# A hybrid RWKV-7 layer on one core: gathered blocks in two buffers, their scaling on VectorE, and seven products that nothing reads in the recurrence's merge

## The chip, the cores and the metric

The kernel runs on one core of a Trainium2 chip. The metric is the device time of one execution in microseconds (us), as the median of three runs. A profiled execution gives the trace from which the rows below come.

## What is computed

One decoder layer for 4096 tokens of 1024 channels in float32. The reference, cut to its steps:

```python
proj = x @ w_in
pool_out = multiscale_pool(proj[..., :256], pool_w, pool_scale)
rwkv_out = rwkv7_mix(proj[..., 256:], ...)        # 12 heads of 64
mixed = concat([pool_out, rwkv_out]) @ w_out
h = layer_norm(alpha * x + mixed)
y = layer_norm(alpha * h + hierarchical_moe(h))   # top group of 4, two of its 8 experts

# inside rwkv7_mix, per head and token; state is 64 x 64
sa = einsum('bhij,bhj->bhi', state, -kk)
state = state * decay + sa * (kk * a) + v * k
out = einsum('bhij,bhj->bhi', state, r)
# afterwards: a norm over each head, + sum(r * k * r_k) * v (the bonus), * a gate
```

## The kernel before, in words

The program has four phases, and the trace shows them one after the other: `phase_project` (to about 1060 us; x @ w_in, each float32 operand split in a high and a low part), `phase_rwkv` (1060 to 2432 us; the recurrence), `phase_out` (w_out, the first layer norm, the router), `phase_moe` (the experts and the last norm).

The recurrence is computed in chunks of 64 tokens. A **unit** is 256 tokens (4 chunks) of one of two groups of 6 heads (3 pairs), so there are 16 x 2 = 32 units. Inside a chunk the tokens depend on one another through a triangular 64x64 matrix for each head, which has to be inverted. Each unit goes through these pieces:

- `load` reads r, k, v and the decays; `gate` computes the low-rank products; `prep` builds the scaled operands AR and KB (VectorE lines 383 to 434), multiplies them on TensorE (L443) and masks the products into G (L445, VectorE). G is written to DRAM (L450, SyncE's queue).
- At the end of `prep` stands `invert`. Four DMAs gather the 32x32 diagonal blocks of G from DRAM, 24 partitions each, into a tile `gi` of 96 partitions (L481), which has one buffer. GpSimd (POOL) scales a unit matrix and the blocks by the norms rn (L483 writes `db`, 96x512; L484 scales `gi`, 96x1024) and then inverts the blocks by elimination: 31 steps, each one multiplication (L489) and one addition (L491).
- `merge` puts the inverses together: `db` goes to DRAM (L500) and back as `ut` (L506), VectorE transposes a part (L509 writes `w`), 24 tiny products (L521), ACT copies the result into W (L529), 24 more (L524), VectorE copies into Uf (L531). With that the 64x64 inverses stand in `ut`.
- `values`, `tail` and `chunk` run the recurrence, chunk by chunk. A `chunk` has three pieces: products of the state with AR (L592, L597), the products with the inverse (L601, with L575 of the next chunk between them), the update of the state (L608 on TensorE, L610 and L611 on VectorE) and the output (L613).
- `bonus` computes the sum of r, k and r_k times v (L462, L469, L470); `post` the norm over a head, the gate and the write of the result.

The engines' order is written out by hand. Every piece is a generator that stops at places (`yield`); tables of ticks (`LOAD`, `GATE`, `PREP`, `BONUS`, `MERGE`, `POST`, `TAIL`, `VALUES`, `CHUNK`) give each stop a tick, with 96 ticks to a unit and 24 to a chunk. All pieces are sorted by tick and recorded one after the other, and each engine works through its own instructions in this order; DMAs stand in the queue of the engine that issues them, most of them SyncE's (SP). An instruction that waits holds up all that stands behind it on its engine.

At the start of `phase_out` the tables that the router and the experts fill later get their first content: 128 rows of zeros for `d_h` and `d_acc` (0.5 MB each), 1 MB of `d_tab`, and `d_gtab`. The weights w_out come in pieces of 512 KB through a pool of two buffers (`o_ws`), issued by ACT, between whose loads ACT also issues the norm's and router's parameters.

Of the kernel before, what the change touches and what calls it, by code (L numbers as in the profile page):

```python
# [27 lines left out]

def phase_project(tc, A, rkv, lora, mixT, xsp):


    nc = tc.nc
# [5 lines left out]
    with ExitStack() as ctx:  # L38
# [38 lines left out]
        def cols(g):  # L77
# [4 lines left out]
            return c  # L82

        wpool = ctx.enter_context(tc.tile_pool(name="pj_wr", bufs=1))
        for g in range(2):
# [110 lines left out]

LOAD = [-5, 92]
GATE = [-63]
PREP = [-76, -70, -67, -67, -62, -62, -55, -55, -48, -36, -31, -31, -30, -23, -17, -15, -15, -15, -13, -7, 3, 4, 7, 7, 7, 7, 8, 28, 30, 30]
BONUS = [7, 13, 19]  # L200
MERGE = [50, 82, 94, 94, 101, 101]
POST = [-2, -2, 11, 11, 20, 23, 35, 37, 49, 50, 57, 60, 62]
TAIL = [-1]
VALUES = [-43]
CHUNK = [0, 6, 12]

def phase_rwkv(tc, A, rkv, lora, mixT, gsc, dsc, rsc):
# [8 lines left out]
    with ExitStack() as ctx:  # L216
# [136 lines left out]
        def prep(n):  # L353
# [493 lines left out]
def bcast_row(ap, n):  # L847

    return bass.AP(tensor=ap.tensor, offset=ap.offset, ap=[[0, 128], [1, n]])


def phase_out(tc, A, mixT, hrow, acc, tab, gtab, plan):
# [3 lines left out]
    with ExitStack() as ctx:  # L856

        wop = ctx.enter_context(tc.tile_pool(name="o_wo", bufs=1))
        cst = ctx.enter_context(tc.tile_pool(name="o_c", bufs=1))
        wst = ctx.enter_context(tc.tile_pool(name="o_w", bufs=2))  # L860
        mp = ctx.enter_context(tc.tile_pool(name="o_m", bufs=3))
# [63 lines left out]
        nc.gpsimd.iota(token, pattern=[[128, NQ]], base=0, channel_multiplier=1)  # L925

        z = cst.tile([128, D], F32, name="zrow")
        nc.gpsimd.memset(z, 0.0)
        nc.sync.dma_start(hrow[S:], z)
        nc.sync.dma_start(acc[S:], z)  # L930
        ft = cst.tile([128, 128, 2], I32, name="ft")
        nc.gpsimd.memset(ft, 0)
        nc.gpsimd.iota(ft[:, :, 0], pattern=[[1, 128]], base=S, channel_multiplier=0)
        tv = tab.rearrange("(a p r) c -> a p r c", p=128, r=128)
        for a in range(NE * CAP // (128 * 128)):
            nc.sync.dma_start(tv[a], ft)
        fg = cst.tile([128, 128], I32, name="fg")
        nc.gpsimd.iota(fg, pattern=[[1, 128]], base=S, channel_multiplier=0)
        nc.sync.dma_start(gtab.rearrange("(p r) c -> p (r c)", r=128), fg)

        def first(QB, eq, pos, n):
# [688 lines left out]
def body(tc, A, out):  # L1630
    with tc.tile_pool(name="dram", bufs=1, space=bass.MemoryType.DRAM) as dp:
# [43 lines left out]
```

## Time and profile before

| | us |
|---|---|
| median of three runs | 3805.84 |
| the three runs | 3802.25, 3805.84, 3812.07 |
| the profiled execution | 3845.02 |
| its span, first to last instruction | 3843.4 |
| PE busy in the span | 3346.6 (87%) |
| VectorE (DVE) busy | 2041.7 (53%) |
| GpSimd (POOL) busy | 1728.8 (45%) |
| ScalarE (ACT) busy | 1600.2 (42%) |
| mean granted clock of TensorE | 0.888 |

The span and the busy times are of the profiled execution, which took longer than the runs without a profile; durations below are from it. PE is TensorE. In the trace a float32 product of the program stands as two records, a transposition as one, so seven products are fourteen records. The granted clock is a share of full speed: 1.00 is 2.4 GHz, 0.50 is 1.2 GHz. "Idle before" a group is time in which its engine did nothing, with the instruction or DMA that ended it.

### The profile page before, as it was taken

The numbers are of one execution on the slowest core, as the hardware profiler recorded it, in microseconds if no ns is written. First come the engines' busy times: TensorE is split into PE (matmuls) and PEld (weight loads), VectorE is DVE, ScalarE is ACT, GpSimd is POOL, SyncE is SP. The second block draws the span as 40 slices with busy tenths as digits, with TensorE's granted clock in tenths as the row PEclk, the third lists the DMA queues.
The fourth block names the chain that finished last, engine by engine and source line by source line (L and its number), as shares of the span: only waits on it lengthen the run. The fifth ranks groups of instructions, "written<-read, shape, count | busy, mean of one in ns | idle before, by whom it ended". The sixth has DMA issues, their size and how long they took to land. (4 is left out here: it accounts for less than half of the span.)

```text
span 3843.4 us, 70576 instructions
## 1 busy us (share of the span) xinstructions
PE 3346.6 (87%) x27405; PEld 2800.3 (73%) x27405; DVE 2041.7 (53%) x4105; ACT 1600.2 (42%) x2694; POOL 1728.8 (45%) x2988
## 2 busy tenths in 40 slices
PE   7999999999948888888888887699894899989993
PEld 6887887777737777777677776588673789878873
DVE  3212231212146676676676774456465555867885
ACT  2212111111134554545545543466553455655552
POOL 3000030000047777777787776133333233645564
PEclk9999999999967877878778777899996899999997
DMA  7434252323133343333333322557643688989993
GB/s 258 175 121 173 112 186 93 130 93 134 45 77 74 71 89 70 76 83 69 80 80 72 87 67 51 181 141 167 132 127 108 166 231 240 288 231 281 270 286 116
DMA packets 509606, 531.21 MB, mean 138 GB/s; under 512 B 297707, under 2 KB 411541, under 8 KB 505174
## 3 DMA queue, kind: packets, MB, share of 16 engines
q1 hardware_dynamic: 445606, 367.94, 33.5%
q0 software_dynamic: 33920, 106.02, 10.7%
q10 hardware_dynamic: 29744, 52.73, 3.7%
q8 instruction: 216, 3.54, 0.4%
q14 instruction: 120, 0.98, 0.1%
HBM read 324.90 MB, written 206.92 MB: 138 GB/s over the span
## 5 line engine op out<-in xcount | busy, mean ns | idle before, releaser
L134 PE MATMUL acc<-xhi,wh 128*128 128x512 f32 x1408 | 565.8, 402 | 4.2 <-DVE zo L176 3.9
L135 PE MATMUL acc<-xlo,wh 128*128 128x512 f32 x1408 | 559.6, 397 | 0.0
L136 PE MATMUL acc<-xhi,wl 128*128 128x512 f32 x1408 | 559.2, 397 | 0.0
L491 POOL TENSOR_TENSOR db<-db,tmp 96x126 f32<-96x126 f32 (+22 forms) x992 | 453.1, 457 | 77.8
L176 DVE SCALAR_TENSOR_TENSOR zo<-acc,omu,zm 128x512 f32<-128x512 f32 x160 | 120.0, 751 | 660.8 <-ACT zm L173 617.2
L489 POOL TENSOR_TENSOR tmp<-db,gi 96x126 f32<-96x126 f32 (+22 forms) x992 | 430.0, 433 | 77.7
L173 ACT ACTIVATE zm<-acc,muc 128x512 f32<-128x512 f32 x160 | 110.2, 690 | 718.9 <-PE acc L136 717.6
L174 POOL COPY carry<-zm 128x1 f32<-128x1 f32 x160 | 30.8, 193 | 663.8 <-ACT zm L173 663.8
L134 PEld LDWEIGHTS acc<-xhi,wh 128*128 128x128 f32 x1408 | 265.4, 189 | 70.9 <-DVE zo L176 4.2
L135 PEld LDWEIGHTS acc<-xlo,wh 128*128 128x128 f32 x1408 | 265.6, 189 | 66.4 <-issue 3.8
L136 PEld LDWEIGHTS acc<-xhi,wl 128*128 128x128 f32 x1408 | 265.5, 189 | 63.5
L1070 PE MATMUL o_ps<-owh,mh 128*128 128x512 f32 x512 | 212.5, 415 | 20.5 <-ACT owh L892 18.5
L1260 POOL DMA_INDIRECT xg<-d_h,ix x81 | 87.4, 1079 | 296.7 <-PE m_pt L1296 288.0
L445 DVE TENSOR_TENSOR g<-tr,mask 128x384 f32<-128x384 f32 x256 | 130.5, 551 | 144.1 <-PE tr L443 144.1
L1070 PE MATMUL o_ps<-owl,mh 128*128 128x512 f32 x512 | 204.0, 400 | 3.0 <-issue 2.7
L1070 PE MATMUL o_ps<-owh,ml 128*128 128x512 f32 x512 | 205.3, 401 | 0.7 <-POOL ml L879 0.7
L443 PE MATMUL tr<-ar,kb 64*128 64x128 f32 x1536 | 180.3, 367 | 24.2 <-DVE kb L430 16.6
L443 PEld LDWEIGHTS tr<-ar,kb 64*128 64x128 f32 x1536 | 149.0, 254 | 45.6 <-DVE g L445 17.0
L1282 POOL DMA_INDIRECT d_acc<-y,ix x81 | 126.7, 1564 | 91.7 <-ACT y L1351 79.7
L370 ACT ACTIVATE thw<-tr,chans 128x256 f32<-128x256 f32 x96 | 45.6, 475 | 293.3 <-PE tr L369 293.3
L1369 PE MATMUL p_y<-wh_d,hh 128*128 128x512 f32 (+1 forms) x324 | 147.6, 455 | 19.3 <-ACT hh L1344 18.5
L879 POOL TENSOR_TENSOR ml<-m,mh 128x1024 fp32r<-128x1024 f32 x32 | 76.6, 2395 | 184.4 <-ACT mh L878 184.3
(362 smaller groups left out, 8929.7 us busy)
## 6 DMA issues: line engine op xcount, KB each, us to landing
d_rkv<-zo SPq DMA_DIRECT2D x144, 256.0 KB
ws<-in_exp_gate_dram SPq DMA_DIRECT2D x64, 512.0 KB
ws<-in_exp_up_dram SPq DMA_DIRECT2D x64, 512.0 KB
ws<-in_exp_down_dram SPq DMA_DIRECT2D x64, 512.0 KB
xq<-in_x_dram SPq DMA_DIRECT2D x32, 512.0 KB
d_xsp<-xhi ACTq DMA_DIRECT2D x8, 2048.0 KB
d_xsp<-xlo ACTq DMA_DIRECT2D x8, 2048.0 KB
xlo<-d_xsp SPq DMA_DIRECT2D x8, 2048.0 KB
```

What stands on the lines that cost most here:

```text
L134: nc.tensor.matmul(ps, lhsT=whi[i][:, k, :], rhs=xhi[:, k, :], start=k == 0, stop=False)
L135: nc.tensor.matmul(ps, lhsT=whi[i][:, k, :], rhs=xlo[:, k, :], start=False, stop=False)
L136: nc.tensor.matmul(ps, lhsT=wlo[i][:, k, :], rhs=xhi[:, k, :], start=False, stop=k == KD - 1)
L173: nc.scalar.activation(zm[:, 1:], ps, AF.Copy, scale=muc[:, ix:ix + 1])
L176: nc.vector.scalar_tensor_tensor(zo, ps, omu[:, ix:ix + 1], zm[:, :SEG], op0=OP.mult, op1=OP.add)
L443: nc.tensor.matmul(ps[h][:, p, :], lhsT=KB[hs, i, :], rhs=AR[hs, i, :], start=True, stop=True)
L445: nc.vector.tensor_tensor(G[:, h, c::NC, :], ps[h], masks[c % 2].unsqueeze(1).to_broadcast([128, 3, 128]), op=OP.mult)
L489: e.tensor_tensor(tm, Dh[:, :a, x:x + 1].to_broadcast([96, a, b]), G[:, x, x + 1:].unsqueeze(1).to_broadcast([96, a, b]), op=OP.mult)
L491: e.tensor_tensor(Dh[:, :a, x + 1:], Dh[:, :a, x + 1:], tm, op=OP.add)
L1070: nc.tensor.matmul(ps, lhsT=a[:, k, :], rhs=w[k][:, ns], start=k == 0 and i == 0, stop=k == KD - 1 and i == 2)
L1282: st = nc.gpsimd.indirect_dma_start(out=acc, out_offset=bass.IndirectOffsetOnAxis(ap=ix[:n, 0:1], axis=0), in_=y[:n], in_offset=None, boun ...
L1369: nc.tensor.matmul(ps[j][:a1 - a0], lhsT=x[:, a0:a1], rhs=w[:, f, n * 512:n * 512 + 512], start=f == 0 and i == 0, stop=f == NF - 1 and i ...
```

## The change

1. `invert` is split. The gather is now `blocks`, recorded in a piece of its own (tick 33) ahead of the inversion (tick 46), and its tile `gi` has two buffers.
2. The scaling of the unit matrix and of the blocks (96x512 and 96x1024) is done by VectorE instead of POOL.
3. `busy` puts products into the merge that nothing reads: four of 128x256 ahead of the first 24 tiny products and three ahead of the second 24, into the tile that these then overwrite. All four last pieces of the merge stand at one tick (100, before 94 and 101), behind the first piece of the next unit's first chunk.
4. The copies of Uf go from VectorE to ACT.
5. The bonus multiplies r by k once for all three pairs; the factor r_k, before part of this step, is now in a constant matrix `rsum`, built once, in place of the matrix of ones.
6. The tables of ticks have new values.
7. In `phase_out` the pool of w_out has four buffers instead of two, and six loads of parameters are issued by SyncE instead of ACT. The first fill of `d_h`, `d_acc`, `d_tab` and `d_gtab` moves to `phase_project`, where it is written behind the first load of the second column group.

The core of the diff:

```diff
@@ phase_project
             load_x(0)
+            if g:
+                empty(hrow, acc, tab, gtab)
...
-LOAD = [-5, 92]
-GATE = [-63]
...
-BONUS = [7, 13, 19]
-MERGE = [50, 82, 94, 94, 101, 101]
...
-CHUNK = [0, 6, 12]
+WARM = [4, 3]
+LOAD = [-14, 73]
+GATE = [-110]
...
+BONUS = [7, 14, 20]
+MERGE = [56, 84, 100, 100, 100, 100]
...
+CHUNK = [0, 6, 14]
...
+        rsum = cst.tile([128, NPAIR, 128], F32, name="rsum")
+        for q in range(NPAIR):
+            nc.vector.tensor_scalar(rsum[:, q, :], ones, rkc[:, q:q + 1], None, op0=OP.mult)
...
-            invert(n, rn)
+            Gi = blocks(n)
+            yield
+            invert(n, rn, Gi)
...
-            for p in range(3):
-                q = 3 * g + p
-                nc.vector.scalar_tensor_tensor(k2[:, p, :], r[:, p, :], rkc[:, q:q + 1], k2[:, p, :],
-                                               op0=OP.mult, op1=OP.mult)
+            nc.vector.tensor_tensor(k2, r, k2, op=OP.mult)
...
-                    nc.tensor.matmul(ps[:, p, :], lhsT=ones, rhs=k2[:, p0 + p, :], start=True, stop=True)
+                    nc.tensor.matmul(ps[:, p, :], lhsT=rsum[:, 3 * g + p0 + p, :], rhs=k2[:, p0 + p, :], start=True, stop=True)
...
+        def blocks(n):
+
+            G = pr.tile([96, 32, 32], F32, name="gi", bufs=2)
             for f in range(2):
                 for b in range(2):
                     o = slice(b * 32, b * 32 + 32)
                     q = f * 48 + b * 24
                     nc.sync.dma_start(G[q:q + 24], gsc[n].rearrange("h i s t -> (h i) s t")[:, o, o])
+            return G
...
-            e.tensor_tensor(Dh, eye, rn.unsqueeze(1).to_broadcast([96, 16, 32]), op=OP.mult)
-            e.tensor_tensor(G, G, rn.unsqueeze(1).to_broadcast([96, 32, 32]), op=OP.mult)
+            nc.vector.tensor_tensor(Dh, eye, rn.unsqueeze(1).to_broadcast([96, 16, 32]), op=OP.mult)
+            nc.vector.tensor_tensor(G, G, rn.unsqueeze(1).to_broadcast([96, 32, 32]), op=OP.mult)
...
+        def busy(ps, n):
+
+            for _ in range(n):
+                nc.tensor.matmul(flat(ps)[:, :256], lhsT=ones, rhs=flat(smask)[:, :256], start=True, stop=True)
...
                 ps = [ptr.tile([128, CP, 32], F32, name="tr") for _ in range(2)]
+                busy(ps[0], WARM[s])
...
-                        nc.vector.tensor_copy(Uf[q0, :, 32:], ps[j][q0])
+                        nc.scalar.activation(Uf[q0, :, 32:], ps[j][q0], AF.Copy)
...
-        wst = ctx.enter_context(tc.tile_pool(name="o_w", bufs=2))
+        wst = ctx.enter_context(tc.tile_pool(name="o_w", bufs=4))
...
-        nc.scalar.dma_start(g1, bcast_row(A["ln1_g"], D))
+        nc.sync.dma_start(g1, bcast_row(A["ln1_g"], D))
```

Three places show how instructions move. Names of the kernel before and after differ in their lines: L445, L610, L611, L383, L416, L419 of before are L468, L642, L643, L406, L439, L442 of after.

On SyncE's queue, the first of the four gathers of a unit, before and after (the names behind "waits" are the semaphores that it waits for):

```order
L481 DMA gi<-d_gsc 24x32x32 [waits DMAHW6_49,DMAHW7_49,DMAHW5_49,Pool_49]
...
L502 DMA gi<-d_gsc 24x32x32 [waits DMAHW2_49,DMAHW1_49,DMAHW0_49]
```

Before, it waits for POOL (the inversion that reads the one buffer); after, for DMAs alone.

On VectorE, around the masking of G (`g`), the scan (`thw<-smask`) and the updates of the state (`st`, the two groups of heads alternate), before:

```order
L445 TENSOR_TENSOR g<-tr,mask_6818 128x3x128 x2
L445 TENSOR_TENSOR g<-tr,mask_6824 128x3x128 x2
L649 TENSOR_TENSOR y<-y,ra 128x768
L610 TENSOR_TENSOR st_6890<-pn,st_6892 128x192
L611 TENSOR_TENSOR st_6890<-st_6890,pc 128x192
L383 SCALAR_TENSOR_TENSOR thw<-smask,thw 128x256 x3
L659 TENSOR_TENSOR yT<-yT,bv 128x768
L668 TENSOR_TENSOR yT<-yT,tr 128x512
L610 TENSOR_TENSOR st_6892<-pn,st_6890 128x192
```

and after:

```order
L468 TENSOR_TENSOR g<-tr,mask_6836 128x3x128 x2
L468 TENSOR_TENSOR g<-tr,mask_6842 128x3x128 x2
L642 TENSOR_TENSOR st_6915<-pn,st_6917 128x192
L643 TENSOR_TENSOR st_6915<-st_6915,pc 128x192
L681 TENSOR_TENSOR y<-y,ra 128x768
L406 SCALAR_TENSOR_TENSOR thw<-smask,thw 128x256 x3
L509 TENSOR_TENSOR db<-eye,rn 96x512
L510 TENSOR_TENSOR gi<-gi,rn 96x1024
L642 TENSOR_TENSOR st_6917<-pn,st_6915 128x192
L643 TENSOR_TENSOR st_6917<-st_6917,pc 128x192
```

The two scalings (L509, L510) now stand between the scan and the state update of the third chunk.

On TensorE, from the end of a unit's last chunk to the next unit's first inverse, before:

```order
L608 MATMUL pn<-rs_6887,kbT 64x64 x6
L613 MATMUL pzr<-rs_6887,g 64x64 x6
L521 MATMUL tr<-w,g 32x32 x24
L551 MATMUL tr<-rw_id,kb 128x128 x3
L592 MATMUL pza<-st_6894,ar 64x64 x6
L597 MATMUL pzr<-st_6894,ar 64x64 x6
L524 MATMUL tr<-ut_6885,w 32x32 x24
L562 MATMUL tr<-cen,ld_v 128x128 x3
L601 MATMUL pza<-z,ut_6885 64x64
```

and after:

```order
L640 MATMUL pn<-rs_6912,kbT 64x64 x6
L645 MATMUL pzr<-rs_6912,g 64x64 x6
L583 MATMUL tr<-rw_id,kb 128x128 x3
L624 MATMUL pza<-st_6919,ar 64x64 x6
L629 MATMUL pzr<-st_6919,ar 64x64 x6
L522 MATMUL tr<-smask,ones 128x256 x4
L553 MATMUL tr<-w,g 32x32 x24
L522 MATMUL tr<-smask,ones 128x256 x3
L556 MATMUL tr<-ut_6910,w 32x32 x24
L594 MATMUL tr<-cen,ld_v 128x128 x3
L633 MATMUL pza<-z,ut_6910 64x64
```

Both groups of the merge (L553, L556) now stand behind the first products of the chunk, each behind products without a reader (L522). The fill of the tables, though written in the second column group, stands on SyncE's queue among the first loads of x at the program's start.

## Rows read from the trace of the kernel before

**Rows 1.** Costliest groups, POOL in the recurrence: busy, mean ns | idle before

```profile
L491 POOL TENSOR_TENSOR db<-db,tmp 96x126 f32<-96x126 f32 (+22 forms) x992 | 453.1, 457 | 77.8
L489 POOL TENSOR_TENSOR tmp<-db,gi 96x126 f32<-96x126 f32 (+22 forms) x992 | 430.0, 433 | 77.7
L484 POOL TENSOR_TENSOR gi<-gi,rn 96x1024 f32<-96x1024 f32 x32 | 76.8, 2400 | 140.6 <-DMA gi<-d_gsc 140.6
L483 POOL TENSOR_TENSOR db<-eye,rn 96x512 f32<-96x512 f32 x32 | 42.3, 1323 | 24.0 <-DVE rn L434 24.0
```

**Rows 2.** Line L484 alone: ns min/median/max, first and last start

```profile
L484 POOL TENSOR_TENSOR gi<-gi,rn x32: 2337/2344/2737, 1111.4 to 2358.6; 96x1024 f32<-96x1024 f32 x32
```

**Rows 3.** Windows: length, busy by engine, clock, DMA share, GB/s

```profile
1240.00:2282.00 1042.00, 878.19 (x12742) 748.76 (x12741) 724.95 (x1525) 540.79 (x1113) 813.42 (x1653) 0.79 0.35 76
5.00:40.00 35.00, 26.26 (x115) 21.27 (x116) 9.86 (x14) 6.82 (x12) 13.42 (x41) 0.95 0.97 332
2432.00:2470.00 38.00, 18.68 (x45) 12.49 (x45) 12.60 (x18) 9.59 (x10) 7.85 (x17) 0.68 0.92 307
```

**Rows 4.** Timeline of DVE, one unit: start, duration [idle before]

```profile
1578.04 0.95 DVE L649 TENSOR_TENSOR y<-y,ra 128x768 f32<-128x768 f32 x1
...
1579.78 2.19 DVE L383 TENSOR_TENSOR_SCAN thw<-smask,thw 128x256 f32<-128x256 f32 x3
...
1595.88 0.57 DVE L509 STREAM_TRANSPOSE w<-ut 96x384 f32<-96x384 f32 x1 [5.71 <-DMA ut<-d_dsc]
...
1599.88 1.30 DVE L427 TENSOR_TENSOR kb<-thw,sq 128x384 f32<-128x384 f32 x2
...
1602.46 1.00 DVE L430 TENSOR_TENSOR kb<-tha,sq 128x384 f32<-128x384 f32 x2
1603.39 0.38 DVE L433 TENSOR_SCALAR rn<-rn 96x32 f32<-96x32 f32 x1
...
1606.97 1.61 DVE L462 SCALAR_TENSOR_TENSOR thw<-ld_r,chans,thw 128x256 f32<-128x256 f32 x3
```

**Rows 5.** Timeline of PE, the same unit

```profile
1579.46 1.13 PE L390 MATMUL tr<-sq,ones 128*128 128x256 f32 x4
...
1596.51 1.49 PE L521 MATMUL tr<-w,g 32*32 32x32 f32 x48 [4.88 <-DVE w L509]
...
1598.76 0.59 PE L592 MATMUL pza<-st,ar 64*64 64x64 f32 x6
...
1599.88 1.49 PE L524 MATMUL tr<-ut,w 32*32 32x32 f32 x48
...
1604.35 2.07 PE L443 MATMUL tr<-ar,kb 64*128 64x128 f32 x14
...
1610.33 2.91 PE L469 MATMUL tr<-thw,ones 128*128 128x256 f32 x6
```

**Rows 6.** Windows of this unit, ahead of and behind PE's wait

```profile
1568.70:1592.60 23.90, 19.86 (x297) 16.44 (x295) 14.99 (x35) 16.66 (x35) 16.71 (x35) 1.00 0.30 53
1592.60:1613.10 20.50, 16.37 (x208) 14.27 (x209) 14.20 (x31) 4.24 (x8) 17.68 (x37) 0.50 0.36 102
```

**Rows 7.** Timeline of POOL and DVE: one shape alone and beside L421

```profile
1582.53 0.30 POOL L491 TENSOR_TENSOR db<-db,tmp 96x56 f32<-96x56 f32 x1
...
1596.23 1.24 POOL L491 TENSOR_TENSOR db<-db,tmp 96x56 f32<-96x56 f32 x1
1596.38 0.91 DVE L421 SCALAR_TENSOR_TENSOR tha<-tha,kx 128x768 f32<-128x768 f32 x1
```

**Rows 8.** Groups of DVE that price what moves

```profile
L423 DVE TENSOR_TENSOR thw<-thw,ld_k 128x768 f32<-128x768 f32 x32 | 34.0, 1063 | 0.0
...
L531 DVE COPY ut<-tr 32x384 f32<-32x384 f32 x64 | 35.2, 551 | 18.1 <-PE tr L524 16.8
```

**Rows 9.** Timeline of the first unit: last masking of G, POOL's start

```profile
1102.14 1.02 DVE L445 TENSOR_TENSOR g<-tr,mask 128x384 f32<-128x384 f32 x2 [0.82 <-PE tr L443]
...
1111.40 2.34 POOL L484 TENSOR_TENSOR gi<-gi,rn 96x1024 f32<-96x1024 f32 x1 [17.35 <-DMA gi<-d_gsc]
```

**Rows 10.** Group of L1070, first products of the output phase

```profile
L1070 PE MATMUL o_ps<-owh,mh 128*128 128x512 f32 x512 | 212.5, 415 | 20.5 <-ACT owh L892 18.5 <-issue 1.9
```

More of the change, by code (lines that the diff above doesn't have):

```diff
@@ L26, in identity, with phase_project @@
                             pattern=[[-1, t.shape[1]]], channel_multiplier=1)
-def phase_project(tc, A, rkv, lora, mixT, xsp):
+def phase_project(tc, A, rkv, lora, mixT, xsp, hrow, acc, tab, gtab):
     nc = tc.nc
@@ L82, in cols, with empty @@
             return c
+        def empty(hrow, acc, tab, gtab):
+            z = cst.tile([128, 256], F32, name="zrow")
+            nc.gpsimd.memset(z, 0.0)
+            for t in (hrow, acc):
+                nc.sync.dma_start(t[S:].rearrange("p (a d) -> p a d", d=256), z.unsqueeze(1).to_broadcast([128, 4, 256]))
+            ft = cst.tile([128, 128, 2], I32, name="ft")
+            nc.gpsimd.memset(ft, 0)
+            nc.gpsimd.iota(ft[:, :, 0], pattern=[[1, 128]], base=S, channel_multiplier=0)
+            tv = tab.rearrange("(a p r) c -> a p r c", p=128, r=128)
+            for a in range(NE * CAP // (128 * 128)):
+                nc.sync.dma_start(tv[a], ft)
+            fg = cst.tile([128, 128], I32, name="fg")
+            nc.gpsimd.iota(fg, pattern=[[1, 128]], base=S, channel_multiplier=0)
+            nc.sync.dma_start(gtab.rearrange("(p r) c -> p (r c)", r=128), fg)
         wpool = ctx.enter_context(tc.tile_pool(name="pj_wr", bufs=1))
@@ L195 @@
 ST = 24 * NC
-LOAD = [-5, 92]
-GATE = [-63]
-PREP = [-76, -70, -67, -67, -62, -62, -55, -55, -48, -36, -31, -31, -30, -23, -17, -15, -15, -15, -13, -7, 3, 4, 7, 7, 7, 7, 8, 28, 30, 30]
-BONUS = [7, 13, 19]
-MERGE = [50, 82, 94, 94, 101, 101]
-POST = [-2, -2, 11, 11, 20, 23, 35, 37, 49, 50, 57, 60, 62]
+WARM = [4, 3]
+LOAD = [-14, 73]
+GATE = [-110]
+PREP = [-76, -69, -67, -66, -64, -64, -56, -55, -51, -31, -29, -26, -26, -23, -23, -14, -13, -13, -11, -11, -4, 6, 6, 6, 6, 6, 6, 33, 33, 33, 46]
+BONUS = [7, 14, 20]
+MERGE = [56, 84, 100, 100, 100, 100]
+POST = [8, 11, 15, 25, 25, 32, 40, 42, 57, 57, 66, 72, 73]
 TAIL = [-1]
 VALUES = [-43]
-CHUNK = [0, 6, 12]
+CHUNK = [0, 6, 14]
 def phase_rwkv(tc, A, rkv, lora, mixT, gsc, dsc, rsc):
@@ L468, in bonus @@
                 for p in range(m):
-                    nc.tensor.matmul(ps[:, p, :], lhsT=ones, rhs=k2[:, p0 + p, :], start=True, stop=True)
+                    nc.tensor.matmul(ps[:, p, :], lhsT=rsum[:, 3 * g + p0 + p, :], rhs=k2[:, p0 + p, :], start=True, stop=True)
                 nc.vector.tensor_tensor(bv[:, p0:p0 + m, :], ps[:, :m, :], v[:, p0:p0 + m, :], op=OP.mult)
                 yield
-        def invert(n, rn):
-            e = nc.gpsimd
-            G = pr.tile([96, 32, 32], F32, name="gi")
+        def blocks(n):
+            G = pr.tile([96, 32, 32], F32, name="gi", bufs=2)
             for f in range(2):
@@ L481, in invert @@
                     nc.sync.dma_start(G[q:q + 24], gsc[n].rearrange("h i s t -> (h i) s t")[:, o, o])
+            return G
+        def invert(n, rn, G):
+            e = nc.gpsimd
             Dh = units[n]["D"] = pr.tile([96, 16, 32], F32, name="db", bufs=2)
-            e.tensor_tensor(Dh, eye, rn.unsqueeze(1).to_broadcast([96, 16, 32]), op=OP.mult)
-            e.tensor_tensor(G, G, rn.unsqueeze(1).to_broadcast([96, 32, 32]), op=OP.mult)
+            nc.vector.tensor_tensor(Dh, eye, rn.unsqueeze(1).to_broadcast([96, 16, 32]), op=OP.mult)
+            nc.vector.tensor_tensor(G, G, rn.unsqueeze(1).to_broadcast([96, 32, 32]), op=OP.mult)
             tmp = pr.tile([96, 256], F32, name="tmp")
@@ L906, in phase_out @@
         b1 = wop.tile([128, D], F32, name="b1")
-        nc.scalar.dma_start(g1, bcast_row(A["ln1_g"], D))
-        nc.scalar.dma_start(b1, bcast_row(A["ln1_b"], D))
+        nc.sync.dma_start(g1, bcast_row(A["ln1_g"], D))
+        nc.sync.dma_start(b1, bcast_row(A["ln1_b"], D))
         wr = cst.tile([128, KD, 64], F32, name="wr")
         nc.vector.memset(wr[:, :, NG + NE:], 0.0)
-        nc.scalar.dma_start(wr[:, :, :NG], A["router_group"].rearrange("l (k p) e -> (l p) k e", p=128))
-        nc.scalar.dma_start(wr[:, :, NG:NG + NE], A["router_expert"].rearrange("l (k p) e -> (l p) k e", p=128))
+        nc.sync.dma_start(wr[:, :, :NG], A["router_group"].rearrange("l (k p) e -> (l p) k e", p=128))
+        nc.sync.dma_start(wr[:, :, NG:NG + NE], A["router_expert"].rearrange("l (k p) e -> (l p) k e", p=128))
         br = cst.tile([128, NG + NE], F32, name="br")
-        nc.scalar.dma_start(br[:, :NG], bcast_row(A["router_group_b"], NG))
-        nc.scalar.dma_start(br[:, NG:], bcast_row(A["router_expert_b"], NE))
+        nc.sync.dma_start(br[:, :NG], bcast_row(A["router_group_b"], NG))
+        nc.sync.dma_start(br[:, NG:], bcast_row(A["router_expert_b"], NE))
         both2 = cst.tile([128, NG + NE], F32, name="both2")
@@ L925, in phase_out @@
         nc.gpsimd.iota(token, pattern=[[128, NQ]], base=0, channel_multiplier=1)
[L927 to L939, printed above, removed]
         def first(QB, eq, pos, n):
@@ L1643, in body @@
         restd = dp.tile([128, 4], I32, name="d_rest")
-        phase_project(tc, A, rkv, lora, mixT, xsp)
+        phase_project(tc, A, rkv, lora, mixT, xsp, hrow, acc, tab, gtab)
         phase_rwkv(tc, A, rkv, lora, mixT, gsc, dsc, rsc)
```

## The prediction

> **What bounds the kernel now.** The change touches mainly the recurrence (1060 to 2432 us of the trace), so I read it by its units, of which there are 32. The view of line L484 gives the period: it runs once in a unit, first at 1111.4 and last at 2358.6 us [rows 2], so (2358.6 - 1111.4) / 31 = 40.2 us. Which engine fills these 40.2 us? The costliest groups answer for POOL: L491 453.1 / 32 = 14.2 us in a unit, L489 13.4, the gaps before them (77.8 + 77.7) / 32 = 4.9, L484 2.4, L483 1.3, and 140.6 / 32 = 4.4 of waiting before L484 for the gathered blocks [rows 1]. That is 40.6, all of the period. The mean of a long stretch of the phase leaves room on the others: of 1042 us, PE is busy for 878, DVE for 725 [rows 3], which is 28.0 us of DVE in a unit. So POOL's inversion of the triangular blocks is the bound, and the 4.4 us are on its path: the gather writes the one buffer that the inversion reads until its end. Everybody else waits for POOL at the merge: DVE 5.71 us for the inverses [rows 4], PE 4.88 us for DVE [rows 5]. After that wait PE's granted clock is 0.50 (1.2 GHz) for 20.5 us, where it was 1.00 (2.4 GHz) in the 23.9 us before [rows 6].
>
> **The change, part by part.**
>
> Gather with two buffers, scalings on DVE. POOL loses the wait (4.4), L484 (2.4) and L483 (1.3): 32.5 us are left. What it gets back is contention: an L491 of 96x56 takes 0.30 us, and another of the same shape 1.24, when L421 of DVE begins beside it [rows 7]. DVE's share grows by the block scaling, which I price by L423, 1063 ns for 768 columns [rows 8]: 1.06 x 1024 / 768 = 1.42, and by half of that, 0.7, for the scaling of 512. If POOL stands still for all of these 2.1 us it comes to 34.6; if for none, 32.5. Either way it is 5 us under the old period and no longer the bound by itself. The Trainium skill ("SBUF — State Buffer", Who interferes with whom) says that a DVE instruction with two SBUF inputs contends with a GpSimd instruction that reads SBUF, which speaks against this move. Rows 7 agree with it for L421. By it the upper of the two numbers holds, which only prices the first rival.
>
> DVE's own work: 28.0 + 1.4 + 0.7; the two copies of Uf go to ACT, -35.2 / 32 = -1.1 [rows 8]; three passes of the bonus (1.61 us [rows 4]) become one tensor_tensor of 768 columns, 1.06, so -0.5. Together 28.5. For ACT, busy for 541 of the 1042 us [rows 3], two copies more in a unit are no load, and the reader of Uf waits for one copy as before. The six small operations that prepare the bonus's constants run once, at the phase's start. The 28.5 must fit with its waits in the period.
>
> The wait for the blocks on DVE. The scaling of the blocks stands in DVE's queue right behind the scan, and behind it the state update of the third chunk, for which PE and the next chunk wait. How long does it stand? In the first unit, where nothing was ahead of the gather, the last masked G ends at 1102.14 + 1.02 = 1103.16 and POOL starts on the blocks at 1111.40 [rows 9], so the round trip through DRAM is 8.2 us. DVE's cover is what lies between: from L649 to the end of the scan 1578.04 to 1581.97, that is 3.9 with a state update [rows 4], plus 0.7 for the first scaling. So 8.2 - 4.6 = 3.6, called 3.5. Its ends are 0 (the round trip is shorter where fewer transfers are under way) and 8.2 (the cover is gone).
>
> The merge. It now follows the first piece of the next unit's first chunk and is a chain on PE: L592 and L597 1.1 us (1598.76 to 1599.88), L521 1.5, L524 with L562 and L601/L575 4.5 (1599.88 to 1604.35), and the first half of L443, some 1.9 [rows 5]. These 9.0 us are at 1.2 GHz; at 2.4 GHz they are 4.5. Seven products without a reader come in: 128x256 as those of L390, of which two take 1.13 at 2.4 GHz, and as those of L469, of which three take 2.91 at 1.2 GHz [rows 5]. In a row I take 0.5 each at the high clock and 0.9 at the low: 3.5 or 6.3 us. The three ahead of L524 lie where ACT copies W anyway and cost little, the four ahead of L521 are on the chain. If both halves of the merge, 24 tiny products each, don't halve fully, the chain is 8.6 at the high clock (between 8.0 and 9.1), and 15.3 at the low one. DVE has L427, L430 and two small steps on rn for that time, 1.30 + 1.00 + about 0.8 [rows 4]. It waits 8.6 - 3.1 = 5.5 us for the first block of L443. The clock is the use of the products: the 4.9 us in which PE did nothing ahead of L521 are gone or filled, and I take it that the clock holds. Other waits of DVE (for the second half of L443, for ACT), which the old period hid, I put at 1.4, between 0.5 and 2.
>
> Sum for DVE: 28.5 + 3.5 + 5.5 + 1.4 = 38.9, with the contention of DVE's own instructions some 0.2 more: **39.1 us**, 1.1 less than now. Over 31 periods that is -34 us. With the bounds it goes from 37.5 to 40.3.
>
> Ends of the phase. In the first and the last unit nothing overlaps the scaling: 2.34 us on POOL [rows 9] against 1.42 on DVE, twice, -2.
>
> The output phase. At its start PE is idle for 19.3 of 38 us, DMA is busy for 0.92 and moves 307 GB/s [rows 3]; before L1070 PE waits 18.5 us for the weights [rows 10]. The zero fills, 2.1 MB by their shapes, leave this stretch: 2.1 MB at 307 GB/s are 6.8 us; two more weight buffers and the six small loads that no longer stand among ACT's weight loads add to it. Taken -9, between -5 and -18. The Trainium skill ("DMA: Bandwidth & Descriptors", Issuing engines are not separate DMA queues) says that moving a load to another issuing engine saves only the issuing; by it the six loads bring nothing beyond their issuing, and the term would be the fills' 6.8 alone.
>
> The fills at their new place. The order shows them among the first loads of x, and DMA is busy for 0.97 at 332 GB/s there, PE for 26 of 35 us [rows 3]. 2.1 MB are 6.3 us of transfers on a path that is already full: taken +5, between 0 and 8.
>
> Net: -34 - 2 - 9 + 5 = -40 us. The profiled execution took 3845.0 us, 1.0% above the median of the runs shown, 3805.84. (3845.0 - 40) / 3845.0 = 0.9896, times 3805.84: **3766 us**.
>
> **Rivals.**
>
> A: POOL is the bound. DVE's waits lie beside one another (the blocks arrive before DVE asks, the merge is hidden under the gate's and the post's work), and the period falls to POOL's 34.6. For it: DVE has only 28.5 of work. Against it: PE's chain, on which DVE waits, runs in every unit. -5.6 x 31 = -174, with the -6 of the other parts -180: 3628 us.
>
> B: slower. The clock falls all the same, now in the 3.5 us in which DVE stands at the blocks' scaling with the state update behind it, and PE has nothing. Then the merge's chain and the products run at 1.2 GHz: up to 15.3 - 8.6 = 6.7 us more in a unit; with the clock back midway 4.0. The period is 43.1: +2.9 x 31 - 6 = +84 us, 3889 us. It decides from a period of 40.4 on (6 / 31 above 40.2). For it: a wait of 4.88 us on PE stood ahead of the low clock in before [rows 5, 6], and one of 3.5 may do the same. Against it: there is post and gate work on PE for it.
>
> C: the wait only changes its engine. DVE stands for the blocks as long as POOL did and the merge gives back nothing, so the period stays at 40.2: only the -6 remain, 3800 us. For it: the recurrence runs through DVE's queue, and there is no second way round.
>
> **How the numbers follow.** Forecast 0.50 (own range 3715 to 3803), A 0.14, B 0.20, C 0.16. A measurement of this kernel tells 0.3% from no change, that is 3794 to 3817. Faster: 0.45 of the forecast, A, and 0.03 of C: 0.62. Same: 0.04 of the forecast and 0.13 of C: 0.17. Slower: B and the last of the forecast: 0.21. The range takes in the forecast, C, the half of A that lies above 3625, and the milder quarter of B: 3625 to 3860.
>
> **What would show it.** Right: no wait of POOL for the gather; the scaling's wait on DVE at 2 to 5 us; L521's and L524's groups at about 0.9 instead of 1.5; a clock above 0.9 over the recurrence; a period near 39; PE's wait at L1070 down by about 9. Wrong: a period of 35 with POOL without gaps (A); a clock at 0.5 at the merge (B); a wait of 5 us and more at the scaling (C). If the clock rose over the whole phase, PE's work shrinks by far more than I allow, and the prediction is too slow; if the round trip takes well over 8 us under load, it is too fast.

## The result, and the profile after

The changed kernel takes 3748.25 us (median of four runs, 3740.32 to 3760.13) beside 3806.57 us of the kernel before, measured with it: the ratio is 0.9843, with a 95% interval from 0.9828 to 0.9857. So it is faster by 58 us, or 1.6%; the forecast was 3766 us, faster by 1.0%. The later runs were made in three further series on three chips, in which the kernel before takes 3844.6, 3844.5 and 3841.8 us (its profiled execution of 3845.02 us is like these). Ratios below are therefore always against the kernel before of the same series, and the changed kernel was run once more among them (`a2_after`): 3788.01 us, 0.9841 [0.9818, 0.9865], again 56 us below the kernel before.

The period of a unit, read at the scaling of the blocks as in [rows 2], here at its new line L510 of the changed kernel (nanoseconds min/median/max, first and last start; below it the idle time of its engine until the named release, and how many times):

```profile
L510 DVE TENSOR_TENSOR gi<-gi,rn x32: 1220/1222/1306, 1118.7 to 2294.4; 96x1024 f32<-96x1024 f32 x32
its engine sat idle before it (us, times) until:
  DMA gi<-d_gsc: 144.2, 32
who waited for it (us, times):
  POOL tmp L515: 127.7, 28
```

(2294.4 - 1118.7) / 31 = 37.9 us instead of 40.2. The same recurrence gives 38.2 in `a2_after` and 37.7 in `e6_out_old` (below), so differences of a few tenths between periods say nothing. The wait for the gathered blocks is still there, 144.2 us against the 140.6 of [rows 1], but it is VectorE's now. POOL's groups, which answer to [rows 1], and the two scalings (busy us, mean ns | idle before, releaser):

```profile
L515 POOL TENSOR_TENSOR tmp<-db,gi 96x126 f32<-96x126 f32 (+22 forms) x992 | 469.5, 473 | 254.9 <-DVE gi L510 127.7 <-DMA rn<-d_rsc 47.0 <-DMA d_dsc<-db 4.9
L517 POOL TENSOR_TENSOR db<-db,tmp 96x126 f32<-96x126 f32 (+22 forms) x992 | 448.8, 452 | 77.7
...
L510 DVE TENSOR_TENSOR gi<-gi,rn 96x1024 f32<-96x1024 f32 x32 | 39.2, 1224 | 144.2 <-DMA gi<-d_gsc 144.2
...
L509 DVE TENSOR_TENSOR db<-eye,rn 96x512 f32<-96x512 f32 x32 | 22.2, 694 | 0.0
```

POOL works (469.5 + 448.8) / 32 = 28.7 us in a unit and has small gaps as before, 4.8 to 4.9 us, 33.6 together; it now waits for VectorE (127.7 us), in 28 of the 32 units. It is no longer the bound. The windows of the changed kernel, to be laid beside [rows 3] (length, busy time of PE, PE's weight loads, DVE, ACT, POOL; granted clock, DMA share, GB/s):

```profile
1240.00:2282.00 1042.00, 909.02 (x13997) 764.01 (x13996) 741.38 (x1566) 583.66 (x1226) 794.81 (x1704) 0.92 0.36 81
...
2367.00:2405.00 38.00, 22.47 (x60) 15.97 (x59) 14.31 (x22) 12.36 (x12) 8.97 (x14) 0.66 0.82 265
```

In the recurrence the granted clock rose from 0.79 to 0.92. VectorE is busy for 741.38 / 1042 x 37.9 = 27.0 us in a unit, so it stands for 10.9. The longest waits of that stretch say where (total us, times, longest):

```profile
DVE g L468 <- PE tr L466: 159.9, 105, 6.0
...
DVE gi L510 <- DMA gi<-d_gsc: 116.4, 27, 5.4
```

1042 us are 27.5 units: 5.8 us in a unit for TensorE's blocks of G behind the merge, 4.2 for the gathered blocks; 0.9 is left for all else. In VectorE's timeline two units follow one another like this (start, duration, what, [idle before and its end]):

```profile
1716.30 0.68 DVE L509 TENSOR_TENSOR db<-eye,rn 96x512 f32<-96x512 f32 x1
1720.78 1.22 DVE L510 TENSOR_TENSOR gi<-gi,rn 96x1024 f32<-96x1024 f32 x1 [3.81 <-DMA gi<-d_gsc]
1721.93 0.35 DVE L642 TENSOR_TENSOR st<-pn,st 128x192 f32<-128x192 f32 x1
...
1756.94 1.22 DVE L510 TENSOR_TENSOR gi<-gi,rn 96x1024 f32<-96x1024 f32 x1 [4.14 <-DMA gi<-d_gsc]
...
1774.75 0.56 DVE L468 TENSOR_TENSOR g<-tr,mask 128x384 f32<-128x384 f32 x1 [5.45 <-PE tr L466]
```

The state update L642 stands right behind the wait for the blocks, as the order had shown. TensorE around the second of these waits and in the merge (L522 are the products that nothing reads; eight records are four products):

```profile
1758.88 0.39 PE L624 MATMUL pza<-st,ar 64*64 64x64 f32 x6 [2.13 <-DVE st L643]
...
1765.94 2.95 PE L522 MATMUL tr<-smask,ones 128*128 128x256 f32 x8
1768.83 0.95 PE L553 MATMUL tr<-w,g 32*32 32x32 f32 x48
1769.70 1.56 PE L522 MATMUL tr<-smask,ones 128*128 128x256 f32 x6
1771.19 0.95 PE L556 MATMUL tr<-ut,w 32*32 32x32 f32 x48
```

and the windows of the same place, which answer to [rows 6]:

```profile
1757.50:1761.10 3.60, 2.14 (x51) 1.80 (x51) 3.46 (x7) 1.61 (x4) 2.33 (x7) 1.00 0.41 64
1761.10:1767.90 6.80, 6.03 (x56) 5.10 (x57) 6.77 (x12) 2.19 (x5) 6.09 (x10) 0.50 0.38 95
1767.90:1774.00 6.10, 6.10 (x140) 5.01 (x140) 1.37 (x4) 2.76 (x7) 5.16 (x13) 1.00 0.66 221
```

TensorE waits 2.13 us for the state that stands behind the scaling, has 2.14 us of work in 3.6, and the clock falls to 0.50 (1.2 GHz). During the four products it comes back to 1.00 (2.4 GHz), so both groups of the merge take 0.95 us, not the 1.49 of [rows 5]. Where [rows 6] had 20.5 us at the low clock, this unit has 6.8; a stretch of 6 to 10 us at the low clock stands in 12 of the 16 units from 1240 to 1840 us.

The two traces differ by 105 us, more than the times. From the last write of the result of the recurrence, they are

```profile
L670 SPq DMA_DIRECT2D d_mix<-yT x32: 359/382/405, 1232.3 to 2432.9; - x32
```

in the kernel before, at 2432.9 of a span of 3843.4 us, and in the changed kernel

```profile
L702 SPq DMA_DIRECT2D d_mix<-yT x32: 359/381/1402, 1236.4 to 2368.0; - x32
```

at 2368.0 of 3738.7: 65 us are gained up to here, and 40 behind it (1410.5 us against 1370.7). The 40 are not the change: `a2_after`, the same program, has 2375.0 of a span of 3786.8, so 1411.8 us behind the recurrence, and the kernels below that share this code take 1392.7 to 1418.9 there. Beside the trace of before, `a2_after` gains 57.9 us up to here and nothing behind it, about as much as its times say.

The last sign that the prediction named is TensorE's wait for the weights at the first products of the output phase, 18.5 us in [rows 10]:

```profile
L1087 PE MATMUL o_ps<-owh,mh 128*128 128x512 f32 x512 | 209.7, 410 | 14.5 <-ACT owh L924 14.5
```

It is down by 4 us (by 5 in `a2_after`: 13.6), where the text had about 9.

### The profile page after: what moved, and what is told of

Read it like the earlier page. It is cut to its first block, busy times and chain, and to the rows that moved or that the text cites. A ratio compares the mean times of both kernels' runs of the same rounds, so it can differ in the third digit from the quotient of the medians.

```text
span 3738.7 us, 71544 instructions
## 1 busy us (share of the span) xinstructions
PE 3314.4 (89%) x27853; PEld 2762.5 (74%) x27853; DVE 2014.2 (54%) x4047; ACT 1617.2 (43%) x2758; POOL 1643.5 (44%) x2924
## 5 line engine op out<-in xcount | busy, mean ns | idle before, releaser
L515 POOL TENSOR_TENSOR tmp<-db,gi 96x126 f32<-96x126 f32 (+22 forms) x992 | 469.5, 473 | 254.9 <-DVE gi L510 127.7
L517 POOL TENSOR_TENSOR db<-db,tmp 96x126 f32<-96x126 f32 (+22 forms) x992 | 448.8, 452 | 77.7
L468 DVE TENSOR_TENSOR g<-tr,mask 128x384 f32<-128x384 f32 x256 | 130.9, 553 | 184.5 <-PE tr L466 184.0
L466 PE MATMUL tr<-ar,kb 64*128 64x128 f32 x1536 | 138.3, 295 | 47.7 <-DVE g L468 27.4
L466 PEld LDWEIGHTS tr<-ar,kb 64*128 64x128 f32 x1536 | 113.0, 192 | 66.0 <-DVE g L468 39.9
L1351 PE MATMUL p_gu<-xl,wh_g 128*128 128x256 f32 (+4 forms) x512 | 153.7, 300 | 0.0
L1351 PE MATMUL p_gu<-xh,wl_g 128*128 128x256 f32 (+4 forms) x512 | 153.6, 300 | 0.0
```

The costliest lines, as they stand in the source:

```text
L466: nc.tensor.matmul(ps[h][:, p, :], lhsT=KB[hs, i, :], rhs=AR[hs, i, :], start=True, stop=True)
L468: nc.vector.tensor_tensor(G[:, h, c::NC, :], ps[h], masks[c % 2].unsqueeze(1).to_broadcast([128, 3, 128]), op=OP.mult)
L1351: nc.tensor.matmul(p[:, :N], lhsT=a[:, k, fs], rhs=c[:, k, :N], start=k == 0 and i == 0, stop=k == KD - 1 and i == 2)
```

## The experiments

The three series hold e1, e2, e3 and e5; a2, e4, e6 and e8; e9 to e12. In each table row or diff the base is the changed kernel unless said otherwise. Periods are read at the scaling of the blocks, from one trace of each kernel.

| run | what | us | ratio to before, 95% | period |
|---|---|---|---|---|
| a2_after | the changed kernel | 3788.01 | 0.9841 [0.9818, 0.9865] | 38.2 |
| e1_no_products | no products | 3799.6 | 0.9892 [0.9864, 0.9920] | 38.7 |
| e3_one_buffer | one buffer | 3859.79 | 1.0060 [1.0039, 1.0082] | 40.1 |
| e2_scale_pool | both scalings on POOL | 3752.53 | 0.9775 [0.9748, 0.9802] | 37.2 |
| e8_split | the blocks' scaling on POOL | 3762.0 | 0.9776 [0.9752, 0.9801] | 37.1 |
| e5_late_scale | scalings behind the state update | 3766.03 | 0.9811 [0.9784, 0.9838] | 37.0 |
| e4_double | 8 and 6 products | 3862.25 | 1.0044 [1.0029, 1.0059] | 40.8 |
| e9_four | 2 and 2 products | 3731.19 | 0.9713 [0.9689, 0.9737] | 36.4 |
| e6_out_old | output phase and fills as before | 3791.07 | 0.9861 [0.9843, 0.9879] | 37.7 |
| e10_split_four | e8 with 2 and 2 products | 3755.09 | 0.9771 [0.9741, 0.9802] | 37.4 |
| e11_split_late_w | e8, inverses transposed later | 3764.29 | 0.9806 [0.9779, 0.9832] | 37.2 |
| e12_late_both | e5, inverses written and transposed later | 3762.36 | 0.9799 [0.9773, 0.9825] | 37.2 |

**Is the second buffer what frees POOL?**

```diff
-            G = pr.tile([96, 32, 32], F32, name="gi", bufs=2)
+            G = pr.tile([96, 32, 32], F32, name="gi")
```

> The changed kernel with one buffer for the gathered blocks. The gather then waits for the end of GpSimd's inversion, on SyncE's queue, and the scaling on VectorE stands behind it, with the state update behind that. Theory 1: the two buffers are needed for the gain. The path becomes inversion (28.7 + 4.9 us), gather (about 5 us), scaling 1.2 to 1.9: 40 us and more in a unit; in these us VectorE and TensorE stand too, and the granted clock falls after it: 40 to 43 us, +65 to +160 us (3815 to 3910). Rival: the inversion is over before the gather wants to go (it has slack of 4 us in the changed kernel), and nothing changes: 3735 to 3760.

Theory 1 holds, at its lower end: 1.006 and a period of 40.1. VectorE's wait for the blocks grows (the group's row in this run):

```profile
L510 DVE TENSOR_TENSOR gi<-gi,rn 96x1024 f32<-96x1024 f32 x32 | 39.1, 1222 | 194.2 <-DMA gi<-d_gsc 194.2
```

6.1 us in a unit instead of 4.5. On SyncE's queue the gather waits for POOL's inversion again (1240 to 2240 us), which it does not in the changed kernel:

```profile
SPq L502 <- POOL db L517: 38.6, 21, 2.5
```

Without the second buffer all other edits together are not faster than the kernel before, but 0.6% slower. In this order of the instructions the second buffer carries 2.2 of the 100 parts of the time. No run puts it alone into the kernel before, so that it would do by itself is not shown; nor is what the copies of Uf, the bonus and the new ticks bring each.

**What do the products bring?**

```diff
-WARM = [4, 3]
+WARM = [0, 0]
```

> The changed kernel without its seven products that nothing reads (both counts 0); all else as changed. Theory 1: the products hold the granted clock at 1.00 over the merge. Without them the clock falls to 0.50 there, the two groups of tiny products (L553, L556) go from 0.95 us back to about 1.5, and the mean period of a unit, 37.9 us in the changed kernel, rises to 38.5 to 40: +20 to +65 us against the changed kernel (3765 to 3815). Rival: the clock holds without them, now that the merge no longer waits for VectorE, and they only lengthen the merge's chain, four by 1.8 us and three by up to 1.4. Then the period falls by 1.8 to 3.2 us: -55 to -100 us (3650 to 3690).

Theory 1 by the period: 38.7 instead of 37.9 to 38.2. The time is 11.6 us (0.5 of 100 parts) above `a2_after`, with intervals that just touch, so less than the 20 us named. The recurrence in a window of 1000 us (the clock is the number third from the end), and the merge of one unit:

```profile
1240.00:2240.00 1000.00, 876.37 (x12774) 751.51 (x12775) 693.53 (x1471) 555.12 (x1160) 736.33 (x1602) 0.79 0.36 80
```

```profile
1708.63 1.49 PE L553 MATMUL tr<-w,g 32*32 32x32 f32 x48
...
1715.65 2.07 PE L466 MATMUL tr<-ar,kb 64*128 64x128 f32 x14
```

The clock is 0.79 again, as before the change, and the merge and the products of G after it (L466) take as long as in [rows 5], at 1.2 GHz. The clock is the products' doing; what it gives is nearly eaten up by their own time.

> The changed kernel with the products that nothing reads doubled, 8 and 6. Theory 1: they lie on the merge's chain, for which VectorE waits; four more take 1.75 us (8 records took 1.99 us) and three more 1.3 us, so the period grows by 2.5 to 3.0 us and the time by 75 to 95 us. Rival: VectorE's wait for the first block of G has other ends (the merge's copies on ACT), and the clock's remaining stretches at 0.50 go: the period grows by less than 1 us, under 30 us.

Theory 1: the period grows by 2.6 us, the time by 74, just under the 75 named. The wait for the blocks of G behind the merge, over the 25 units of 1240 to 2260 us:

```profile
DVE g L468 <- PE tr L466: 232.7, 100, 9.0
```

9.3 us in a unit against 5.9 in `a2_after` (159.8 us in 27 units). The products are on the chain, and beyond seven they buy no clock: 0.92 in this run as with seven. The other direction is left to try:

```diff
-WARM = [4, 3]
+WARM = [2, 2]
```

> The changed kernel with two and two products that nothing reads, instead of four and three. By the runs so far, seven more products cost 2.6 us in a unit (period 40.76 against 38.18) and none at all cost 0.8 us more than none saves (38.71 against 37.92 to 38.18), so the seven bring some 3.2 us by the clock and take 2.6. Theory: the clock wants PE to be busy over the whole wait, and four products keep part of it: 37.9 to 38.7 in the period, 0 to +20 us against the changed kernel's 3788 of the call before. Rival: four are enough for the clock and save 3 x 0.37 = 1.1 us: period 37.0, -35 us.

The theory falls and the rival holds, by more than it said: 0.9713, period 36.4, 57 us below `a2_after`. This is the fastest of all kernels, and its interval lies below that of the changed kernel. Four products keep the clock as well as seven (0.93), and the wait behind the merge shrinks, over 28 units:

```profile
1240.00:2240.00 1000.00, 866.60 (x13844) 725.66 (x13836) 754.45 (x1576) 583.90 (x1227) 798.00 (x1711) 0.93 0.38 85
```

```profile
DVE g L468 <- PE tr L466: 107.3, 83, 4.3
```

107.3 / 28 = 3.8 us instead of 5.9. In its timeline two products ahead of L553 take 1.06 us (1709.53 to 1710.59); at the 0.37 us that a product cost in `e4_double`, three fewer give 1.1 of the 2.1 us, and where the rest comes from no run shows:

```profile
1709.53 1.13 PE L522 MATMUL tr<-smask,ones 128*128 128x256 f32 x4
1710.59 0.95 PE L553 MATMUL tr<-w,g 32*32 32x32 f32 x48
```

**Do the scalings belong on VectorE?**

```diff
-            nc.vector.tensor_tensor(Dh, eye, rn.unsqueeze(1).to_broadcast([96, 16, 32]), op=OP.mult)
-            nc.vector.tensor_tensor(G, G, rn.unsqueeze(1).to_broadcast([96, 32, 32]), op=OP.mult)
+            e.tensor_tensor(Dh, eye, rn.unsqueeze(1).to_broadcast([96, 16, 32]), op=OP.mult)
+            e.tensor_tensor(G, G, rn.unsqueeze(1).to_broadcast([96, 32, 32]), op=OP.mult)
```

> The changed kernel with both scalings back on GpSimd; the gather keeps its two buffers and its early place. Theory 1: VectorE's wait for the blocks (144.2 / 32 = 4.5 us in a unit) with the state update behind it is on the path, so taking it off VectorE helps there, but GpSimd gets 2.4 + 1.3 us back on top of 28.7 of work and 4.9 of gaps: 37.3 us, and becomes the bound. Period 37.3 to 38, time within 20 us of the changed kernel (3730 to 3770). Rival: VectorE's queue was not the bound and GpSimd has no slack left; the period goes to 40 as in the kernel before, +65 us (3815). A second rival: GpSimd's part runs faster without VectorE's two-input scalings beside it, and the period is 35 to 36: -60 to -90 us (3660 to 3690).

The period is 37.2, at the edge of theory 1; the time is 35 us below `a2_after`, with disjoint intervals, which theory 1 did not give. POOL is now without slack: (448.7 + 445.9 + 80.7 + 42.1) / 32 + 4.9 = 36.7 us of 37.2.

```profile
L517 POOL TENSOR_TENSOR db<-db,tmp 96x126 f32<-96x126 f32 (+22 forms) x992 | 448.7, 452 | 77.7
L515 POOL TENSOR_TENSOR tmp<-db,gi 96x126 f32<-96x126 f32 (+22 forms) x992 | 445.9, 449 | 77.7
...
L510 POOL TENSOR_TENSOR gi<-gi,rn 96x1024 f32<-96x1024 f32 x32 | 80.7, 2521 | 35.4 <-DMA gi<-d_gsc 35.4
...
L509 POOL TENSOR_TENSOR db<-eye,rn 96x512 f32<-96x512 f32 x32 | 42.1, 1317 | 24.8 <-DVE rn L457 24.6 <-DVE yT L700 0.2
```

So with seven products the changed kernel does better without the move of the scalings. VectorE gains nothing by giving them up:

```profile
1240.00:2240.00 1000.00, 869.83 (x13522) 729.29 (x13520) 723.37 (x1469) 567.48 (x1202) 855.25 (x1707) 0.94 0.37 82
```

It is busy for 723.37 / 1000 x 37.2 = 26.9 us in a unit, where the changed kernel has 27.0 with the scalings. Of the 1.9 us that it is spared, (69.1 - 36.0) / 32 = 1.0 comes back in L439, whose group in this run and in the changed kernel is

```profile
L439 DVE TENSOR_TENSOR ar<-ld_r,p 128x384 f32<-128x384 f32 x64 | 69.1, 1118 | 9.1 <-ACT p L425 7.9 <-PE pzr L629 1.1
...
L439 DVE TENSOR_TENSOR ar<-ld_r,p 128x384 f32<-128x384 f32 x64 | 36.0, 604 | 5.2 <-ACT p L425 4.3 <-PE pzr L629 0.9
```

The kernel before shows the cause. Its L416 (the same two operations) beside POOL's scaling of the blocks, and in the next unit, where the two do not meet:

```profile
1630.54 2.35 POOL L484 TENSOR_TENSOR gi<-gi,rn 96x1024 f32<-96x1024 f32 x1 [3.72 <-DMA gi<-d_gsc]
1631.04 2.78 DVE L416 TENSOR_TENSOR ar<-ld_r,p 128x384 f32<-128x384 f32 x2 [0.65 <-PE pzr L597]
...
1669.28 1.03 DVE L416 TENSOR_TENSOR ar<-ld_r,p 128x384 f32<-128x384 f32 x2 [0.65 <-PE pzr L597]
```

VectorE is through 0.9 us after POOL's scaling ends (1632.89), instead of 1.03 us after its own start. All nine units of before in which L416 takes more than 1.5 us (2.5 to 3.2), and all 17 such units of `e2_scale_pool`, have this scaling beside it.

The blocks' scaling alone on POOL does the same as both:

```diff
-            nc.vector.tensor_tensor(G, G, rn.unsqueeze(1).to_broadcast([96, 32, 32]), op=OP.mult)
+            e.tensor_tensor(G, G, rn.unsqueeze(1).to_broadcast([96, 32, 32]), op=OP.mult)
```

> The changed kernel with the scaling of the blocks back on GpSimd and the scaling of the unit matrix left on VectorE. Theory: the wait for the blocks no longer stands in VectorE's queue, as with both scalings on GpSimd, and GpSimd carries 28.2 + 4.9 + 2.5 = 35.6 us instead of that run's 36.9, so it is the bound at a period of 35.6 to 36.5: 45 to 70 us less than the changed kernel of this call. Rival: the floor of VectorE and TensorE lies at 37 us, as with both scalings on GpSimd (37.25): -20 us.

The rival holds: 37.1, though POOL has 1.3 us less to do. In this kernel POOL waits for the gathered blocks (60.0 us in 7 units), VectorE for the inverses (1240 to 2260 us):

```profile
DVE w L540 <- DMA ut<-d_dsc: 89.4, 23, 7.9
```

**Is the wait for the blocks on the path?**

```diff
-PREP = [..., 33, 33, 33, 46]
+PREP = [..., 33, 33, 33, 63]
```

> The changed kernel with the scalings and the inversion put at tick 63 instead of 46, behind the state update of the third chunk; the gather stays at tick 33. VectorE then asks for the blocks some 6 us later. Theory 1: the wait for the blocks (4.5 us in a unit) is on the path, and the stretches at a granted clock of 0.50 that follow it in 12 of 15 units (6.8 us each) come from it: both go. The period falls by 3 to 4.5 us, to the 35.2 us of a unit without a low clock and below; GpSimd's 33.6 us are the floor: -75 to -130 us (3620 to 3675). Rival: the inversion ends too late for the merge, and the wait moves to the transposition of the inverses (L540, DMA of ut): within 20 us of the changed kernel or slower (3730 to 3790).

Both in part. The wait for the blocks is gone, from 144.2 to 24.9 us:

```profile
L510 DVE TENSOR_TENSOR gi<-gi,rn x32: 1211/1222/1411, 1119.2 to 2267.4; 96x1024 f32<-96x1024 f32 x32
its engine sat idle before it (us, times) until:
  DMA gi<-d_gsc: 24.9, 21
```

and units of 32 to 35 us appear, as theory 1 said, but every other unit takes 36 to 47, because the inverses now come late and VectorE stands for them (1240 to 2260 us):

```profile
DVE w L540 <- DMA ut<-d_dsc: 63.2, 14, 7.0
```

The mean period is 37.0, the time 22 us below `a2_after`; the intervals overlap, so a gain in time is not shown.

Three tries to get further from there by later places for the inverses or fewer products did not work. In `e12_late_both` the merge's first stops went from 56 and 84 to 64 and 90, in `e11_split_late_w` the second from 84 to 90, `e10_split_four` has two and two products.

> As the kernel with both scalings on VectorE at tick 63 (period 37.04, units of 33 and of 42 us in turn), with the write of the inverses at tick 64 instead of 56 and their transposition at 90 instead of 84. Theory: there VectorE stood for the inverses (L540, 63.2 us in 14 units) and the gather stood behind their write on SyncE's queue; with both later, GpSimd's 33.6 us and VectorE's 28.5 have room, and the units come evenly: 34.5 to 36: -35 to -75 us against 3766 (3690 to 3730). Rival: the inversion itself is too late for the merge, 33.6 us after tick 63 and 7 us through DRAM; then the merge waits, the units stay uneven and the period stays at 37 or above: 3750 to 3800.

> As the kernel with the blocks' scaling alone on GpSimd (period 37.14), with the transposition of the inverses (L540) put behind the state update of the fourth chunk (tick 90 instead of 84). In that kernel VectorE waits 89.4 us in 23 units for the inverses with the state update behind it. Theory: that wait is on the path of the recurrence, as the wait for the blocks was; without it the period falls to GpSimd's 35.7 to 36.4: -25 to -45 us (3717 to 3737). Rival: the inverses are late whatever stands in the queue, the merge needs them, and nothing changes: 3750 to 3775.

> As the kernel with the blocks' scaling alone on GpSimd (period 37.14), with two and two products. There the merge waits for the inverses (L553 for L540, 58.8 us in 17 units) and GpSimd is near its bound. Theory: GpSimd sets the pace, so fewer products change little: 37.0 to 37.5, within 15 us of that kernel's 3762. Rival: the products lie on the path there too, three fewer save 1.1 us: -35 us.

The rivals of the first two hold, and the theory of the third. With the transposition later, TensorE waits for it in every unit instead (`e11_split_late_w`, 27 units):

```profile
PEld tr L553 <- DVE w L540: 69.3, 27, 5.6
```

In all six kernels in which the blocks' wait is out of VectorE's queue, or nearly so (e2, e5, e8, e10 to e12), the period is 37.0 to 37.4, and the merge waits for the inverses. That the inverses come too late there is shown; in `e2_scale_pool` POOL's 36.7 us nearly fill the period, but why the others close at 37 and not at POOL's 33.6 to 35.6 us is not settled. With two and two products the answer on the scalings turns round: the changed order (`e9_four`, 0.9713 [0.9689, 0.9737]) is then faster than with the blocks' scaling on POOL (`e10_split_four`, 0.9771 [0.9741, 0.9802]), if by little more than the intervals.

**Output phase and fills.**

The edit takes `phase_out` from the kernel before and leaves out the fill in `phase_project`.

> The changed kernel with the output phase and the fills as in the kernel before: fills back at the start of the output phase, two weight buffers, six loads from ACT. Theory: the fills cost 4.9 us in the projection's first segment (its products reach the 384th at 133.3 us instead of 128.3) and their move with the buffers brings 4 to 9 us in the output phase. The two nearly cancel: 0 to +5 us against the changed kernel of this call. Rival: the changed output phase brings all of the 40 us that the first pair of traces differs by behind the recurrence: +35 us.

The theory holds: 3 us apart, the intervals overlap, so neither a gain nor a loss in time is shown. Both halves can be seen. The first scaling of the recurrence starts at 1112.0 us here and at 1117.8 in `a2_after`, so the fills cost some 5.8 us at the program's start. In the first 38 us of the output phase TensorE works 19.17 us here and 24.13 in `a2_after`, and its wait for the weights is 18.0 us here and 13.6 there, so 4 to 5 us come back:

```profile
2353.00:2391.00 38.00, 19.17 (x47) 12.38 (x48) 13.37 (x17) 10.77 (x11) 6.92 (x11) 0.69 0.94 309
```

```profile
2375.00:2413.00 38.00, 24.13 (x63) 17.26 (x64) 14.29 (x22) 13.47 (x13) 9.03 (x9) 0.63 0.85 271
```

## Why the prediction was right, and where it was off

- **The bound.** POOL with a gather that waits for it: right. With one buffer the period is 40.1, with two POOL is no longer the bound (33.6 us in a unit, between the 32.5 and 34.6 of the text). The contention was argued wrongly. POOL's two groups did grow, by (918.3 - 883.1) / 32 = 1.1 us, but POOL cannot stand still beside the scaling of the blocks when it has nothing to do: in 28 of 32 units it is idle and waits for this scaling. With both scalings on POOL the groups are 894.6, still 0.4 us in a unit above before; which of VectorE's operations lengthen them otherwise, no run separates. The contention of VectorE's own operations, put at 0.2 us more, went the other way: L416 takes 2.78 us beside POOL's scaling and 1.03 us without it, and the move of the scalings takes this neighbour away. The Trainium skill ("SBUF — State Buffer", Who interferes with whom) says that a VectorE instruction with two SBUF inputs contends with a GpSimd instruction that reads SBUF; these rows agree.
- **VectorE's own work** was put at 28.5 us and is 27.0. The step that was mis-sized is not what moved: the two scalings cost 0.69 and 1.22 us against 0.7 and 1.4. I carried the 28.0 of before over unchanged, and some of its operations became shorter, L416 most: its mean is 837 ns before and 604 ns after, at the line L439, which is (51.0 - 36.0) / 32 = 0.5 us in a unit. What had stretched it is POOL's scaling of the blocks, which the change removes. The rest of the 1.5 is spread over smaller differences.
- **The wait for the blocks**: 3.5 put, 4.2 to 4.5 measured. The round trip held; a little less lay between.
- **The merge's chain**: 5.5 us of waiting put, 5.8 measured; L553 and L556 at 0.95 us as said. The products' price, 0.5 us each, is what three of them take at the high clock (1.56 us above); doubling them showed that it is paid, at 2.6 / 7 = 0.37 us for each one more.
- **The rest**: 1.4 put, 0.9 measured. 27.0 + 4.2 + 5.8 + 0.9 = 37.9, where the text had 39.1: 1.2 us in 31 units, 37 us in the trace. VectorE's 1.5 and the rest's 0.5 went one way, the two waits' 1.0 the other, so that the sum came this close is in part luck.
- **The clock.** I took it that it holds from the products on. It holds in the merge, but falls in most units for about 7 us behind the wait for the blocks, as rival B said of the place. B's price was wrong: it had the low clock last through half of the merge, and the four products end it before L553.
- **Output phase and fills**: net -4 put, about 0 measured (4 to 5 back where 9 were put, 5.8 paid where 5 were).
- **What I did not see**: that the move of the scalings to VectorE, which I priced as a gain of POOL's time, is with seven products a loss of 0.7 of 100 parts, since POOL had room for them once the gather was free (`e2_scale_pool`, and `e8_split` with the blocks' scaling alone); with two and two products it is not. And that four products do better than seven, since each one more lengthens the chain and here buys no clock.

## What to carry to other kernels

Here the transfer waited for the reader of its one buffer, and the second buffer was the edit without which nothing was gained; moving the work behind it to another engine put the same wait in another queue, where the state update stood behind it. Whether such a move pays can turn with another edit, here with the number of products, so try it again after each. Products that only hold the clock pay by the clock and cost by the chain, so try half and double. Read a gain by the period of the loop in one trace and by times measured side by side, because two traces of the same code may differ by 1%.

## What was not expected of the hardware

Four products of 128x256 in a merge keep the mean granted clock as high as seven or fourteen do (0.93, 0.92 and 0.92 over 1000 us of the recurrence), and none leave it at 0.79. Two VectorE operations of 128x384 that met a POOL operation of 96x1024 ended only after it (2.78 us instead of 1.03). The kernel before takes 3806.6 us in the first series and 3842 to 3845 us in the three others; the likely cause, another chip, is not shown.
